# Two state-space layers: decay clamp moved from VectorE to ScalarE, the masked product of C and B in one pass, half of the products one weight piece later

## The chip, the cores and the metric

The kernel runs on one core of a Trainium2 chip. The metric is the device time of one execution in microseconds (us). The kernel before takes 2148.89 us, the median of three runs (2148.83 to 2150.71).

Engines are named as the profile names them: PE is TensorE's matmul, PEld its weight load, DVE is VectorE, ACT is ScalarE, POOL is GpSimd, SP is SyncE.

## The reference

A network of four layers on 256 tokens of width 1024, in 32-bit floats. Each layer is a gated feed-forward block, a mixer, and a second feed-forward block, with a layer norm behind each. The mixers of layers 0 to 3 are: state space, attention with a forget gate, block attention, state space. Only the state-space mixer (`mamba2_mixer`) is touched here:

```python
zxbcdt = x @ w_in
z, xbc, dt = split(zxbcdt)                     # 2048, 2048 + 2*4*128, 32 columns
xbc = silu(causal_conv4(xbc) + conv_b)         # then xs, b, c
dt = softplus(dt + dt_bias);  a = -exp(a_log)
# per group g of 4, with 8 heads of 64 columns, state size 128
a_cs = cumsum(dt * a)
decay_in[l, s] = exp(a_cs[l] - a_cs[s])  for s <= l, else 0
cb = c[l] . b[s]
y = (cb * decay_in) @ (x * dt)                 # the diagonal terms
y = y + x * d_skip
y = y * silu(z)
y = y * rsqrt(mean(y^2 over the group) + eps) * norm_w
out = y @ w_out
```

The 256 tokens are one chunk for the reference. The kernel computes them as two halves of 128: the second half gets its own triangle (the diagonal terms) and the contribution of the first half through the state of the first half (the off-diagonal term).

## The kernel before, in words

**Tiles and streams.** Every weight matrix is cut into pieces of 128x2048 floats. SP loads a piece into a raw tile, ACT copies it to a rounded tile `wh` and DVE subtracts that from the raw tile to give the rest `wl` (`split`, L122 to L124, four passes of 128x512 on each engine for each piece). Each product is three matmuls, `wh` by `xh`, `wl` by `xh` and `wh` by `xl` (L148 to L150). The 256 tokens are two streams of 128, t=0 (the first tokens) and t=1 (the second tokens). Both use the same piece, t=1 two pieces after t=0 (`LAG` is 2).

**The state-space mixer.** `ssm` is a generator for one stream. Its pieces come in the order X0 Z0 X1 Z1 O0 X2 Z2 X3 O1 Z3 O2 O3: X is three pieces of the group (two for x, one for B and C), Z and O are two. Stage functions are attached to pieces by `at(i, f, ...)` and run in the code behind the matmuls of piece i:

- `stage_x`, `stage_bc`: the projection is copied out of PSUM (L445 on ACT, L453 on DVE), transposed (L158), put behind the three older tokens (L447, L455 on DVE), and, in the second stream, convolved (L427 on ACT, L431 on DVE) and put through Silu (L434 on ACT).
- `stage_back`: transposes back (L464), the products with dt, the skip and the decay to the end (L469 on DVE), the product of B and C on PE (L478), masked by the triangle on DVE (L481). In the second stream the tile holds two products side by side, of which the second is not masked and is copied by ACT (L483).
- `stage_off`: the off-diagonal matmul (L489), from the first half's state, and its decay (L491, L494 on DVE).
- `stage_m`, twice for each group and stream: a row of cumulated decays is spread over 128 partitions by a DMA, four DVE passes add the partition's own negative value and cut at zero (L502), ACT takes the exponential (L503), DVE multiplies by the masked product (L504). The tiles are named `mt`, five of them.
- `stage_y`: eight matmuls of 64 columns (L512, sixteen records in the profile), added to the skip term on DVE (L514).
- `stage_z`, `stage_n`, `stage_a`: Silu of z on ACT (L519), product (L524), square with a sum on ACT (L526), the scale on DVE and POOL (L527, L528), the scaled result on DVE (L529), transposes (L158) and the split into `ah` and `al` (L123, L124) for the O pieces.

**What sets the order.** The two streams are interleaved piece by piece, and a scheduler orders the instructions of each engine when the program is built; `tc.keep_in_program_order` holds an instruction in the place of the code. Each engine then runs its list in order and waits on semaphores. PSUM has two tiles each of three kinds. Those named `tp` hold transposes and the product of B and C, those named `gu` and `ga` projections and diagonal terms, and those named `acc0` and `acc1` the output sums. ACT loads a table of functions (ACT_TABLE_LOAD) where the next function is not in the one that it has.

Of the kernel before, what the change touches and what calls it, by code (L numbers as in the profile page):

```python
# [7 lines left out]
F32 = mybir.dt.float32  # L8
FR = mybir.dt.float32r
BF = mybir.dt.bfloat16  # L10
AF = mybir.ActivationFunctionType
ALU = mybir.AluOpType
# [37 lines left out]
def build(tc, x, wst, ln_g, ln_b, sm_dt, sm_rows, sm_conv, sm_nw, fx_f, fx_b, out, plan=None):  # L50
    nc = tc.nc
    ctx = ExitStack()
    cpool = ctx.enter_context(tc.tile_pool(name="const", bufs=1))
# [13 lines left out]
    def T():  # L67
        return ps_t.tile([128, 512], F32, name="tp")
# [7 lines left out]
    def tmp(cols, tag, bufs, dt=F32):  # L76
        return spool.tile([128, cols], dt, name=tag, tag=tag, bufs=bufs)
# [6 lines left out]
    K = {}  # L84

    def consts():
        if K:
            return
        up = tmp(128, "t1", 5)
        make_upper_triangular(nc, up, val=1.0, diag=True)  # L90
        lo = tmp(128, "t1", 5)
        make_lower_triangular(nc, lo, val=1.0, diag=False)
        K["tri"] = cpool.tile([128, 128], FR, name="tri")
        nc.vector.tensor_copy(K["tri"], up)
        K["ntri"] = cpool.tile([128, 128], FR, name="ntri")
        nc.vector.tensor_scalar_mul(K["ntri"], up, -1.0)
        K["sel"] = cpool.tile([128, 32], FR, name="sel")
        nc.vector.tensor_add(K["sel"], ident[:, 0:32], ident[:, 32:64])
        K["strict"] = cpool.tile([128, 128], FR, name="strict")
        nc.vector.tensor_copy(K["strict"], lo)  # L100
        K["idb"] = cpool.tile([128, 128], BF, name="idb")
        nc.vector.tensor_copy(K["idb"], ident)
        K["mlo"] = cpool.tile([128, 128], BF, name="mlo")
        nc.vector.tensor_scalar_mul(K["mlo"], lo, NEG)
        K["mup"] = cpool.tile([128, 128], BF, name="mup")
        nc.vector.tensor_sub(up, up, ident)
        nc.vector.tensor_scalar_mul(K["mup"], up, NEG)
# [251 lines left out]
    def ssm_small(j):  # L359
        if j in ssms:  # L360
            return ssms[j]
        consts()
        s = St()
        s.dt = small_w(sm_dt[j], 32)
        s.rows = tmp(96, "rows", 1)
        nc.sync.dma_start(s.rows, bc(sm_rows[j:j + 1, :], 96))
        s.conv = spool.tile([128, 24, 5], F32, name="conv", bufs=1)
        nc.sync.dma_start(s.conv, sm_conv[j])
        s.na = tmp(32, "na", 1)
        nc.scalar.activation(s.na, s.rows[:, 32:64], AF.Exp)  # L370
        nc.vector.tensor_scalar_mul(s.na, s.na, -1.0)
        s.nw = {}
        s.xb, s.cv, s.B, s.xe = {}, {}, {}, {}
        ssms[j] = s
        return s
# [7 lines left out]
    def ssm(st, j):  # L383
        t = st.t
        s = ssm_small(j)
        d = St()
# [12 lines left out]
        def stage_cum():  # L399
            ps = T()  # L400
            nc.tensor.matmul(ps[:, :128], d.h, K["tri"], start=True, stop=False)
            nc.tensor.matmul(ps[:, :128], d.l, K["tri"], start=False, stop=True)
            cr = tmp(128, "cumr", 2)
            nc.scalar.activation(cr[:32], ps[:32, :128], AF.Copy)
            d.cum = dpool.tile([32, 128], F32, name="cums")
            nc.sync.dma_start(d.cum, cr[:32])
            ps = T()
            for n, mat in enumerate(("tri", "strict")[:2 - t]):
                nc.tensor.matmul(ps[:, n * 32:n * 32 + 32], K[mat], d.h[:, :32], start=True, stop=False)
                nc.tensor.matmul(ps[:, n * 32:n * 32 + 32], K[mat], d.l[:, :32], start=False, stop=True)  # L410
            d.ncum = tmp(32, "ncum", 2)
            nc.vector.tensor_scalar_mul(d.ncum, ps[:, :32], -1.0)
            if t == 0:
                d.de = tmp(32, "de", 1)
                nc.scalar.activation(d.de, ps[:, 32:64], AF.Exp)
                nc.vector.tensor_mul(d.de, d.de, d.dt)
            else:
                d.ec = tmp(32, "ec", 1)
                nc.scalar.activation(d.ec, ps[:, :32], AF.Exp)
# [16 lines left out]
        bank, cbs, zss, y1s = {}, {}, {}, {}  # L436
# [13 lines left out]

        def stage_bc(g):
            bcs = tmp(256, "t1", 5)
            nc.vector.tensor_copy(bcs, bank.pop(g)[:, :256])  # L453
            tp = transposes(bcs, 2)
            nc.vector.tensor_copy(s.xb[g][:, 4:6, 3 + t * 128:131 + t * 128], tp[:, :256].rearrange("p (a b) -> p a b", a=2))  # L455
            if t == 1:
                conv(g, 4, 6)

        def stage_back(g):
            cv = s.cv[g]  # L460
            h8 = slice(g * 8, g * 8 + 8)
            tp = T()
            for k in range(4):
                nc.tensor.transpose(tp[:, k * 128:(k + 1) * 128], cv[:, k, mine], ident)  # L464
            tp8 = tp.rearrange("p (a b) -> p a b", a=8)

            def times(tag, rows, bufs):
                o = tmp(512, tag, bufs)
                nc.vector.tensor_mul(o.rearrange("p (a b) -> p a b", a=8), tp8,  # L469
                                     rows[:, h8].unsqueeze(2).to_broadcast([128, 8, 64]))  # L470
                return o
            xds[g] = (times(f"xdt{t}", d.dt, 1 + t), times("xD", s.rows[:, 64:96], 2))
            if t == 0:
                s.xe[g] = times("xe", d.de, 1)
            tp = T()
            for n in range(1 + t):
                B = cv[:, 4, mine if n == 0 else slice(0, 128)]
                nc.tensor.matmul(tp[:, n * 128:(n + 1) * 128], B, cv[:, 5, mine], start=True, stop=True)  # L478
            cb = tmp(256, "t1", 5)
            nn = (1 + t) * 128  # L480
            nc.vector.tensor_mul(cb[:, :128], tp[:, :128], K["tri"].bitcast(F32))  # L481
            if t:
                nc.scalar.activation(cb[:, 128:], tp[:, 128:256], AF.Copy)  # L483
            cbs[g] = cb
            mts[g] = []

        def stage_off(g):
            yo = G()
            nc.tensor.matmul(yo, cbs[g][:, 128:256], s.xe[g], start=True, stop=True)  # L489
            w = tmp(512, "t2", 4)  # L490
            nc.vector.tensor_mul(w.rearrange("p (a b) -> p a b", a=8), yo.rearrange("p (a b) -> p a b", a=8),  # L491
                                 d.ec[:, g * 8:g * 8 + 8].unsqueeze(2).to_broadcast([128, 8, 64]))
            xD = xds[g][1]
            nc.vector.tensor_add(xD, xD, w)  # L494

        def stage_m(g, qd):
            e = spool.tile([128, 4, 128], F32, name="mt", bufs=5)
            h0 = g * 8 + qd * 4
            row = d.cum[h0:h0 + 4, :].rearrange("h l -> (h l)").unsqueeze(0)
            nc.sync.dma_start(e.rearrange("p a b -> p (a b)"), row.to_broadcast([128, 512]))  # L500
            for h in range(4):
                nc.vector.tensor_scalar(e[:, h], e[:, h], d.ncum[:, h0 + h:h0 + h + 1], 0.0, op0=ALU.add, op1=ALU.min)  # L502
            nc.scalar.activation(e, e, AF.Exp)  # L503
            nc.vector.tensor_mul(e, e, cbs[g][:, 0:128].unsqueeze(1).to_broadcast([128, 4, 128]))  # L504
            mts[g].append(e)

        def stage_y(g):
            mt, (xd, xD) = mts.pop(g), xds.pop(g)
            y = G()
            for h in range(8):  # L510
                c64 = slice(h * 64, h * 64 + 64)
                nc.tensor.matmul(y[:, c64], mt[h // 4][:, h % 4], xd[:, c64], start=True, stop=True)  # L512
            y1s[g] = tmp(512, "t2", 4)
            nc.vector.tensor_add(y1s[g], y, xD)  # L514

# [20 lines left out]
        def at(i, f, *a):  # L536
            post.setdefault(i, []).append((f, a))
# [6 lines left out]
        for g in range(N_GRP):  # L544
            b = where["X", g, 2]
            at(b - 1, stage_x, g)
            at(b, stage_bc, g)
            c = b + (LAG if t == 0 else 0)
            at(c + 1, stage_back, g)
            at(c + 2, stage_m, g, 0)  # L550
            at(c + 2, stage_m, g, 1)
            if t == 1:
                at(c + 2, stage_off, g)
            z = where["Z", g, 1]
            at(z, stage_z, g)
            iy = c + 3
            at(iy, stage_y, g)
            n = max(iy, z)
            at(n, stage_n, g)
            at(min(n + 1, where["O", g, 0] - 1), stage_a, g)  # L560
        first_o = where["O", 0, 0]
        for i, (kind, g, n) in enumerate(pieces):
            if (kind == "X" and n != 1) or (kind == "Z" and n == 0):
                ps = bank[g] = GA(int(kind == "Z" or n == 2)) if i < first_o else G()
# [358 lines left out]
```

## Time and profile before

| | before |
|---|---|
| median of three runs | 2148.89 us |
| the profiled execution | 2147.68 us |
| its span in the profile | 2145.9 us |
| PE busy | 2111.0 us (98 %) |
| DVE busy | 1493.1 us (70 %) |
| ACT busy | 1121.4 us (52 %) |
| TensorE clock granted | 0.999 of full speed |

The profiled execution took 2147.68 us, 1.8 us more than the span that its trace covers, and lies 1.2 us below the median. Matmul busy time overlaps from one to the next, so PE's idle time is read better from the table of what PE waited for than from the busy share. In rows of a timeline the first number is the start, the second the duration; `x4` joins four instructions; what stands in brackets is the idle time of the engine before the row and what ended it.

### The profile page before, as it was taken

What the parts mean: (1) busy time and instruction counts of PE and PEld (TensorE: products, weight loads), DVE (VectorE), ACT (ScalarE), POOL (GpSimd) and SP (SyncE); (2) the same over time, 40 slices, a digit from 0 to 9 for tenths busy, and PEclk for the clock granted to TensorE, in tenths of its full rate; (3) what the DMA queues carried; (4) which work ended last, traced back from release to release, by engine and by line L of the source; (5) the groups of instructions that cost most, each with busy time, mean ns of one, the idle gap of its engine ahead of it and who ended that gap; (6) DMA issues with size and microseconds to landing.
All of it is one profiled execution on the core that took longest, in us unless ns stands there. A gap on an engine that the chain in (4) does not pass through costs nothing.

```text
span 2145.9 us, 29868 instructions
## 1 busy us (share of the span) xinstructions
PE 2111.0 (98%) x10346; PEld 1745.7 (81%) x10346; DVE 1493.1 (70%) x2975; ACT 1121.4 (52%) x2298; POOL 476.0 (22%) x858
## 2 busy tenths in 40 slices
PE   8999999999999999999999999999999999999998
PEld 7888878788888888788888887788888888787886
DVE  6657999855765575765675575765576679998655
ACT  6444776544544455544544455544445447665442
POOL 2331000233143200043233300034223310001331
PEclk9999999999999999999999999999999999999999
DMA  9665544666576643466666653376666655446662
GB/s 322 228 228 189 192 167 154 229 234 223 188 261 230 216 167 118 148 233 224 219 229 229 225 200 138 118 248 235 223 216 236 230 203 175 165 173 208 236 228 94
DMA packets 225927, 438.81 MB, mean 204 GB/s; under 512 B 20464, under 2 KB 20976, under 8 KB 225776
## 3 DMA queue, kind: packets, MB, share of 16 engines
q1 hardware_dynamic: 197616, 394.92, 51.3%
q0 software_dynamic: 28160, 41.99, 6.6%
q8 instruction: 81, 1.33, 0.3%
q14 instruction: 70, 0.57, 0.1%
HBM read 414.74 MB, written 22.09 MB: 204 GB/s over the span
## 4 chain that ended last, share of the span: by engine, by line
PE 91%; DVE 4%; ACT 2%; DMA 1%; issue 1%; POOL 0%; DVEq 0%; SPq 0%; ACTq 0%
PE gu L150 16%; PE gu L148 16%; PE gu L149 15%; PE acc L150 9%; PE acc L148 9%; PE acc L149 9%; PE ga L148 4%; PE ga L149 3%; PE ga L150 3%; PE tp L158 3%; DVE wl L124 1%; PE gu L512 1%; DMA raw<-in_w_dram 1%; PE gu L694 1%; DVE mt L502 1%
## 5 line engine op out<-in xcount | busy, mean ns | idle before, releaser
L124 DVE TENSOR_TENSOR wl<-raw,wh 128x512 fp32r<-128x512 f32 x1408 | 887.8, 683 | 361.4 <-ACT wh L123 360.1
L123 ACT ACTIVATE wh<-raw 128x512 fp32r<-128x512 f32 x1408 | 775.2, 621 | 522.2 <-PE gu L150 216.0
L148 PE MATMUL gu<-wh,xh 128*128 128x512 f32 (+1 forms) x1600 | 619.3, 387 | 5.7 <-ACT t L519 2.7
L150 PE MATMUL gu<-wh,xl 128*128 128x512 f32 (+1 forms) x1600 | 617.0, 386 | 0.9 <-DVE xl L124 0.9
L149 PE MATMUL gu<-wl,xh 128*128 128x512 f32 (+1 forms) x1600 | 616.9, 386 | 0.0
L246 POOL DMA_DIRECT2D aT<-turn x640 | 348.3, 551 | 500.0 <-issue 286.4
L148 PEld LDWEIGHTS gu<-wh,xh 128*128 128x128 f32 x1600 | 300.9, 188 | 68.1 <-DVE t L272 3.7
L150 PE MATMUL acc<-wh,al 128*128 128x512 f32 x896 | 352.5, 394 | 0.0
L149 PE MATMUL acc<-wl,ah 128*128 128x512 f32 x896 | 352.4, 393 | 0.0
L148 PE MATMUL acc<-wh,ah 128*128 128x512 f32 x896 | 351.3, 393 | 0.0
L150 PEld LDWEIGHTS gu<-wh,xl 128*128 128x128 f32 x1600 | 300.7, 188 | 61.8 <-DVE xl L124 2.1
L149 PEld LDWEIGHTS gu<-wl,xh 128*128 128x128 f32 x1600 | 300.8, 188 | 59.5 <-issue 0.5
L272 DVE TENSOR_TENSOR t<-t,gu 128x256 f32<-128x256 f32 x176 | 73.6, 418 | 191.3 <-ACT t L270 191.3
L270 ACT ACTIVATE t<-gu 128x256 f32<-128x256 f32 x176 | 67.7, 384 | 258.9 <-PE gu L150 241.1
L150 PEld LDWEIGHTS acc<-wh,al 128*128 128x128 f32 x896 | 168.3, 188 | 37.5 <-DVE al L124 2.3
L148 PEld LDWEIGHTS acc<-wh,ah 128*128 128x128 f32 x896 | 168.3, 188 | 34.9 <-issue 0.5
L149 PEld LDWEIGHTS acc<-wl,ah 128*128 128x128 f32 x896 | 168.3, 188 | 34.6 <-issue 1.3
L242 POOL DMA_DIRECT2D turn<-tb x160 | 90.3, 565 | 321.5 <-DVE tb L240 302.3
L148 PE MATMUL ga<-wh,xh 128*128 128x512 f32 (+1 forms) x448 | 159.6, 358 | 1.4 <-ACT xh L123 1.4
L150 PE MATMUL ga<-wh,xl 128*128 128x512 f32 (+1 forms) x448 | 156.4, 350 | 0.0
L149 PE MATMUL ga<-wl,xh 128*128 128x512 f32 (+1 forms) x448 | 156.1, 349 | 0.0
L190 POOL TENSOR_TENSOR rstd<-ve,mhalf 128x1 f32<-128x1 f32 x24 | 22.6, 942 | 481.5 <-DVE ve L188 481.5
(171 smaller groups left out, 1641.0 us busy)
## 6 DMA issues: line engine op xcount, KB each, us to landing
raw<-in_w_dram SPq DMA_DIRECT2D x351, 1024.0 KB, 5.3
turn<-tb POOLq DMA_DIRECT2D x160, 128.0 KB, 3.3
aT<-turn POOLq DMA_DIRECT2D x640, 32.0 KB, 4.0
mt<-cums SPq DMA_DIRECT2D x32, 256.0 KB, 4.7
gb<-in_ln_g_dram SPq DMA_DIRECT2D x12, 512.0 KB, 4.5
gb<-in_ln_b_dram SPq DMA_DIRECT2D x12, 512.0 KB, 6.0
nw<-in_sm_nw_dram SPq DMA_DIRECT2D x8, 256.0 KB, 5.3
h<-in_x_dram SPq DMA_DIRECT2D x4, 256.0 KB, 4.5
```

The source lines that it names most:

```text
L123: a = nc.scalar.activation(wh, raw, AF.Copy)
L124: return a, nc.vector.tensor_sub(wl, raw, wh.bitcast(F32))
L148: nc.tensor.matmul(o, xh, wh, start=start, stop=False)
L149: nc.tensor.matmul(o, xh, wl, start=False, stop=False)
L150: nc.tensor.matmul(o, xl, wh, start=False, stop=stop)
L158: nc.tensor.transpose(tp[:, j * 128:(j + 1) * 128], src[:, j * 128:(j + 1) * 128], ident)
L190: nc.gpsimd.tensor_tensor(rstd, ve, mhalf, op=ALU.pow)
L242: nc.gpsimd.dma_start(dr, b.rearrange("p q k t -> p (q k t)"))
L246: nc.gpsimd.dma_start(aT[32 * q:32 * q + 32].rearrange("p i k t -> p i (k t)"), dv[q])
L270: nc.scalar.activation(sg, gu[:, :256], AF.Silu)
L272: nc.vector.tensor_mul(a, sg, gu[:, 256:])
L502: nc.vector.tensor_scalar(e[:, h], e[:, h], d.ncum[:, h0 + h:h0 + h + 1], 0.0, op0=ALU.add, op1=ALU.min)
```

## The change

It edits `consts` and five of `ssm`'s stage functions. A constant `cut` of 128x256 (triangle, then ones) lets one DVE pass mask and copy the product of B and C for both streams, and ACT's copy goes. `cums` holds the positive cumulated decays. The clamp of DVE, `min(row - cum, 0)`, becomes ACT's `relu(cum - row)`, and the exponential gets a scale of -1. `stage_bc`'s copy out of PSUM goes from DVE to ACT. The off-diagonal matmul and the first diagonal matmul are held in the order of the code. For the second stream and groups 0 to 2, `stage_m` and `stage_y` are attached one piece later.

```diff
+        K["cut"] = cpool.tile([128, 256], F32, name="cut")
+        nc.vector.tensor_copy(K["cut"][:, 0:128], up)
+        nc.vector.memset(K["cut"][:, 128:256], 1.0)
...
-            d.ncum = tmp(32, "ncum", 2)
-            nc.vector.tensor_scalar_mul(d.ncum, ps[:, :32], -1.0)
+            d.cums = tmp(32, "ncum", 2)
+            nc.vector.tensor_copy(d.cums, ps[:, :32])
...
-            nc.vector.tensor_copy(bcs, bank.pop(g)[:, :256])
+            nc.scalar.activation(bcs, bank.pop(g)[:, :256], AF.Copy)
...
-            nc.vector.tensor_mul(cb[:, :128], tp[:, :128], K["tri"].bitcast(F32))
-            if t:
-                nc.scalar.activation(cb[:, 128:], tp[:, 128:256], AF.Copy)
+            nc.vector.tensor_mul(cb[:, :nn], tp[:, :nn], K["cut"][:, :nn])
...
-            nc.tensor.matmul(yo, cbs[g][:, 128:256], s.xe[g], start=True, stop=True)
+            tc.keep_in_program_order(nc.tensor.matmul(yo, cbs[g][:, 128:256], s.xe[g], start=True, stop=True))
...
-                nc.vector.tensor_scalar(e[:, h], e[:, h], d.ncum[:, h0 + h:h0 + h + 1], 0.0, op0=ALU.add, op1=ALU.min)
-            nc.scalar.activation(e, e, AF.Exp)
+                nc.scalar.activation(e[:, h], e[:, h], AF.Relu, scale=-1.0, bias=d.cums[:, h0 + h:h0 + h + 1])
+            nc.scalar.activation(e, e, AF.Exp, scale=-1.0)
...
-                nc.tensor.matmul(y[:, c64], mt[h // 4][:, h % 4], xd[:, c64], start=True, stop=True)
+                ins = nc.tensor.matmul(y[:, c64], mt[h // 4][:, h % 4], xd[:, c64], start=True, stop=True)
+                if h == 0:
+                    tc.keep_in_program_order(ins)
...
-            at(c + 2, stage_m, g, 0)
-            at(c + 2, stage_m, g, 1)
+            late = int(t == 1 and g < 3)
+            at(c + 2 + late, stage_m, g, 0)
+            at(c + 2 + late, stage_m, g, 1)
...
-            iy = c + 3
+            iy = c + 3 + late
```

Lines of the changed kernel from L98 on carry a number higher by three at first (L148 is L151, L158 is L161, L478 is L481, L489 is L490, L512 is L513), since `cut` takes three lines and the mask's copy gives two back.

In ACT's order the table loads number 40 before and 52 after, six more in each of the two state-space layers.

What the change moves on the engines is seen in the order of their instructions. A row is line, operation, out<-in and shape; numbers behind a name tell tiles of one name apart, and they differ between the two programs.

The first place is PE in layer 0, group 0. The rows named `ga` with 256 columns are the B and C projection of the next group; `tp<-cv` is the product of B and C, whose input `cv` comes from the convolution's Silu. Before:

```order
L149 MATMUL ga_2334<-wl_2220,xh0_1813 128x256
L150 MATMUL ga_2334<-wh_2219,xl0_1814 128x256
L148 MATMUL ga_2334<-wh_2219,xh0_1813 128x256
L149 MATMUL ga_2334<-wl_2220,xh0_1813 128x256
L150 MATMUL ga_2334<-wh_2219,xl0_1814 128x256
L148 MATMUL ga_2334<-wh_2219,xh0_1813 128x256
L149 MATMUL ga_2334<-wl_2220,xh0_1813 128x256
L478 MATMUL tp_2252<-cv_1920 128x128
L464 MATMUL tp_2268<-ident_78,cv_1920 128x128 x4
L478 MATMUL tp_2277<-cv_1920 128x128 x2
L150 MATMUL ga_2334<-wh_2219,xl0_1814 128x256
```

After:

```order
L153 MATMUL ga_2219<-wh_1936,xl1_1978 128x512
L151 MATMUL ga_2336<-wh_2222,xh0_1816 128x256
L152 MATMUL ga_2336<-wl_2223,xh0_1816 128x256
L153 MATMUL ga_2336<-wh_2222,xl0_1817 128x256
L481 MATMUL tp_2255<-cv_1923 128x128
L467 MATMUL tp_2271<-ident_78,cv_1923 128x128 x4
L151 MATMUL ga_2336<-wh_2222,xh0_1816 128x256
L152 MATMUL ga_2336<-wl_2223,xh0_1816 128x256
L153 MATMUL ga_2336<-wh_2222,xl0_1817 128x256
L151 MATMUL ga_2336<-wh_2222,xh0_1816 128x256
L152 MATMUL ga_2336<-wl_2223,xh0_1816 128x256
```

Eleven matmuls of the 256-column projection stood ahead of the first product (the fence shows the last seven), and three do now.

The second place is PE in layer 0, group 1. `tp<-cv ... x2` is the second stream's product of B and C, `gu<-xe,t1` the off-diagonal matmul, for which `t1` is the masked product; `acc0` are output sums. Before:

```order
L150 MATMUL ga_2616<-wh_2373,xl1_1975 128x512
L149 MATMUL acc0_2804<-wl_2554,ah_2520 128x512
L150 MATMUL acc0_2804<-wh_2553,al_2521 128x512
L464 MATMUL tp_2670<-ident_78,cv_2324 128x128 x4
L478 MATMUL tp_2679<-cv_2324 128x128 x2
L489 MATMUL gu_2754<-xe_2652,t1_2682 128x512
L148 MATMUL gu_2725<-wh_2619,xh0_1813 128x512
```

After:

```order
L152 MATMUL acc0_2789<-wl_2450,ah_2595 128x512
L481 MATMUL tp_2681<-cv_2326 128x128 x2
L153 MATMUL acc0_2789<-wh_2449,al_2596 128x512
L151 MATMUL acc0_2789<-wh_2449,ah_2595 128x512
L152 MATMUL acc0_2789<-wl_2450,ah_2595 128x512
L153 MATMUL acc0_2789<-wh_2449,al_2596 128x512
L151 MATMUL acc0_2789<-wh_2542,ah_2599 128x512
L152 MATMUL acc0_2789<-wl_2543,ah_2599 128x512
L490 MATMUL gu_2739<-xe_2654,t1_2684 128x512
L151 MATMUL gu_2726<-wh_2621,xh0_1816 128x512
L152 MATMUL gu_2726<-wl_2622,xh0_1816 128x512
```

The off-diagonal matmul stood directly behind the product, and now six matmuls of the output sums stand between.

The same group on DVE, from the masked product of the second stream to the decay of the off-diagonal term (`t<-gu,ec`) and the row behind it. Before:

```order
L481 TENSOR_TENSOR t_2682<-tp,tri 128x128
L124 TENSOR_TENSOR wl<-raw,wh 128x512 x3
L502 TENSOR_SCALAR mt<-mt,ncum 128x128 x16
L504 TENSOR_TENSOR mt<-mt,t_2656 128x512 x2
L504 TENSOR_TENSOR mt<-mt,t_2682 128x512 x2
L491 TENSOR_TENSOR t_2756<-gu,ec 128x512
L124 TENSOR_TENSOR wl<-raw,wh 128x512
```

After:

```order
L484 TENSOR_TENSOR t_2684<-tp,cut 128x256
L127 TENSOR_TENSOR wl<-raw,wh 128x512 x3
L505 TENSOR_TENSOR mt<-mt,t_2658 128x512 x2
L492 TENSOR_TENSOR t_2741<-gu,ec 128x512
L127 TENSOR_TENSOR wl<-raw,wh 128x512
L495 TENSOR_TENSOR xD<-xD,t_2741 128x512
L127 TENSOR_TENSOR wl<-raw,wh 128x512 x3
L517 TENSOR_TENSOR t_2779<-gu,xD 128x512
L527 TENSOR_TENSOR t_2779<-t_2779,t_2564 128x512
L505 TENSOR_TENSOR mt<-mt,t_2684 128x512
```

Sixteen clamps and two of the four products stood ahead of the decay of the off-diagonal term and now do not: the clamps are ACT's, and the second stream's two products come after it.

The third place is PE in layer 0, group 2. `gu<-xdt1` is the second stream's diagonal product, and `tp<-ident,t2` the transposes of the first stream's normalised result. Before:

```order
L149 MATMUL gu_3248<-wl_2968,xh1_1974 128x512
L150 MATMUL gu_3248<-wh_2967,xl1_1975 128x512
L148 MATMUL gu_3248<-wh_2967,xh1_1974 128x512
L149 MATMUL gu_3248<-wl_2968,xh1_1974 128x512
L150 MATMUL gu_3248<-wh_2967,xl1_1975 128x512
L512 MATMUL gu_3322<-xdt1_3151,mt_3225 128x64 x4
L512 MATMUL gu_3322<-xdt1_3151,mt_3233 128x64 x4
L158 MATMUL tp_3363<-ident_78,t2_3294 128x128 x4
L148 MATMUL gu_3248<-wh_3030,xh1_1974 128x512
```

After:

```order
L153 MATMUL gu_3232<-wh_2968,xl1_1978 128x512
L151 MATMUL gu_3232<-wh_2968,xh1_1977 128x512
L152 MATMUL gu_3232<-wl_2969,xh1_1977 128x512
L153 MATMUL gu_3232<-wh_2968,xl1_1978 128x512
L153 MATMUL acc1_2632<-wh_3163,al_2849 128x512
L151 MATMUL gu_3232<-wh_3031,xh1_1977 128x512
L152 MATMUL gu_3232<-wl_3032,xh1_1977 128x512
L161 MATMUL tp_3346<-ident_78,t2_3278 128x128 x4
L153 MATMUL gu_3232<-wh_3031,xl1_1978 128x512
L151 MATMUL gu_3232<-wh_3031,xh1_1977 128x512
```

The second stream's eight diagonal matmuls stood ahead of those transposes and now come behind them; two more projection matmuls and one of the output sum stand there instead, fifteen large matmuls where there were twelve, counted from the first stream's own diagonal product.

## Rows read from the trace of the kernel before

**Rows 1.** Page, busy time, share of the span and instructions of each engine.

```profile
PE 2111.0 (98%) x10346; PEld 1745.7 (81%) x10346; DVE 1493.1 (70%) x2975; ACT 1121.4 (52%) x2298; POOL 476.0 (22%) x858
```

**Rows 2.** What PE waited for, whole run: total us, times, longest.

```profile
PE gu L489 <- ACT t L483: 2.9, 2, 1.4
PE gu L148 <- ACT t L519: 2.7, 2, 1.4
PE gu L512 <- DVE t L491: 2.1, 2, 1.1
...
PE tp L158 <- DVE t L529: 1.7, 6, 0.5
...
PE gu L148 <- DVE sm L527: 1.0, 2, 0.5
...
PE tp L158 <- DVE al L124: 0.5, 2, 0.2
```

**Rows 3.** Layer 0's mixer by stretch: busy of five engines, clock, DMA, GB/s.

```profile
300.00:320.00 20.00, 18.63 (x99) 15.71 (x99) 19.69 (x54) 17.69 (x30) 0.00 (x0) 1.00 0.44 164
...
sum 151.00, PE 145.59 PEld 124.05 DVE 139.42 ACT 100.63 POOL 5.76; mean PE 24.27 PEld 20.67 DVE 23.24 ACT 16.77 POOL 0.96
```

**Rows 4.** Timeline of DVE in group 1 of layer 0.

```profile
276.30 0.28 DVE L481 TENSOR_TENSOR t<-tp,tri 128x128 f32<-128x128 f32 x1
...
278.30 3.23 DVE L502 TENSOR_SCALAR mt<-mt,ncum 128x128 f32<-128x128 f32 x16
281.44 2.49 DVE L504 TENSOR_TENSOR mt<-mt,t 128x512 f32<-128x512 f32 x4
283.85 0.68 DVE L491 TENSOR_TENSOR t<-gu,ec 128x512 f32<-128x512 f32 x1
```

**Rows 5.** Timeline of PE in the same group.

```profile
276.94 1.12 PE L489 MATMUL gu<-xe,t 128*128 128x512 f32 x2 [1.44 <-ACT t L483]
...
284.59 2.00 PE L512 MATMUL gu<-xdt,mt 128*128 128x64 f32 x16 [1.06 <-DVE t L491]
```

**Rows 6.** Timeline of ACT in group 2 of layer 0.

```profile
308.83 2.08 ACT L427 ACTIVATE cv<-xb,conv 128x256 f32<-128x256 f32 x4 [0.66 <-DVE xb L447]
...
312.22 0.60 ACT L519 ACTIVATE t<-gu 128x512 f32<-128x512 f32 x1
...
329.92 0.60 ACT L519 ACTIVATE t<-gu 128x512 f32<-128x512 f32 x1
```

**Rows 7.** Timeline of PE at the first of these.

```profile
312.87 0.50 PE L148 MATMUL gu<-wh,xh 128*128 128x512 f32 x1 [1.37 <-ACT t L519]
```

**Rows 8.** Timeline of ACT in group 0 of layer 0.

```profile
233.64 1.28 ACT L434 ACT_TABLE_LOAD   x1
234.94 0.63 ACT L434 ACTIVATE cv<-cv 128x512 f32<-128x512 f32 x1
```

**Rows 9.** Timeline of PE in group 0 of layer 0.

```profile
234.42 0.28 PE L148 MATMUL ga<-wh,xh 128*128 128x256 f32 x1
...
235.74 0.38 PE L478 MATMUL tp<-cv 128*128 128x128 f32 x2
```

**Rows 10.** Groups of ACT by line and shape: busy us, mean ns, idle before.

```profile
L427 ACT ACTIVATE cv<-xb,conv 128x256 f32<-128x256 f32 x48 | 25.3, 591 | 5.5 <-DVE xb L447 4.1 <-DVE xb L455 1.3
...
L659 ACT ACTIVATE mt<-tp,rs 128x128 f32<-128x128 f32 x32 | 11.3, 366 | 14.1 <-DVE rs L655 14.1
...
L483 ACT ACTIVATE t<-tp 128x128 f32<-128x128 f32 x8 | 2.2, 272 | 3.9 <-DVE t L481 3.9
```

**Rows 11.** Timeline of DVE at group 2's first normalisation, layer 0.

```profile
335.73 0.69 DVE L514 TENSOR_TENSOR t<-gu,xD 128x512 f32<-128x512 f32 x1 [1.31 <-PE gu L512]
...
339.02 0.75 DVE L529 SCALAR_TENSOR_TENSOR t<-t,sm,nw 128x512 f32<-128x512 f32 x1 [0.67 <-POOL sm L528]
```

**Rows 12.** Timeline of PE beside it.

```profile
333.80 1.89 PE L512 MATMUL gu<-xdt,mt 128*128 128x64 f32 x16
335.53 0.39 PE L158 MATMUL tp<-ident,t 128*128 128x128 f32 x2
...
340.25 0.61 PE L158 MATMUL tp<-ident,t 128*128 128x128 f32 x4
```

## The prediction

> **What bounds the kernel now.** I read the page's busy times first. PE is busy for 98 % of the span, DVE for 70 %, ACT for 52 % [rows 1]. The number of PE's matmuls does not change, so the change can only win or lose in PE's idle time, and the second view is the list of what PE waited for. Six of its rows belong to the two state-space layers: 2.9 us for ACT's copy L483, 2.7 us for the Silu of z (L519), 2.1 us for L491, 1.7 us for the normalised result (L529), 1.0 us for L527 and 0.5 us for a split [rows 2]. Most come twice, once in each layer. They sum to 10.9 us, which is all that the change can give back: 0.5 % of the time.
>
> The third view, by stretch, says why these waits are there. In the 151 us of layer 0's mixer from 197 to 348 us DVE is busy for 139.4 us (92 %) and ACT for 100.6 us (67 %) [rows 3]. The fourth view, DVE's timeline in group 1, shows the queue: 16 clamps, then four products, then L491, each starting before the end of the one ahead [rows 4].
>
> **The load that moves, per layer.** DVE gives 64 clamps at 3.23/16 = 0.20 us, 12.9 us, and 8 copies of 256 columns at about 0.4 (between 0.28 us for 128 columns and 0.69 us for 512 [rows 4, 11]), 3.2 us. It gets 4 masks of double width at +0.14, 0.6 us. So 139.4 - 15.5 = 124 us, 82 %. No row shows a Relu with scale and bias on 128x128. The nearest are a plain copy of that size at 272 ns, an activation with a pointer operand on that size at 366 ns, and one with two pointers on twice the width at 591 ns [rows 10]. Consecutive ones overlap: four L427 take 2.08 us, 0.50 apart, 0.1 less than their mean [rows 6, 10]. So a Relu costs between 0.17 (the copy less 0.1) and 0.49; I take 0.27, the 366 less 0.1. ACT gets 64 x 0.27 = 17.3 us, 8 copies at about 0.3 = 2.4 us and six more table loads at 1.28 [rows 8] = 7.7 us, and loses 4 copies (0.7 us): 100.6 + 26.7 = 127 us, 84 %. With the ends of the Relu it is 121 or 141 us. Both engines would then be fuller than ACT is now and emptier than DVE is now, so I expect no new bound over the whole stretch; the single places decide.
>
> For that one activation the Trainium skill, "ScalarE: Activation LUTs", section "What ACT_TABLE_LOAD costs", gives about 280 ns plus 0.833 ns a column with a bias pointer, and 93 ns of overlap: 387 - 93 = 294 ns as an estimate, 1.5 us more per layer than my sum. Its 1283 ns for a table load is what the trace shows.
>
> **Wait for L483, 2.9 us.** PE waits 1.44 us ahead of L489 [rows 5], until DVE's mask at 276.30 [rows 4] and ACT's copy behind it are done. After the change ACT is out of this chain, and PE has six large matmuls at 0.24 us there, 1.4 us. (0.24 from twelve of them between the transposes at 335.53 and 340.25, less 1.73 us for the eight small ones [rows 12].) PE is free at 276.94 - 1.44 = 275.50, and would arrive at 276.9; the wider mask ends at about 276.3 + 0.42 = 276.7. The wait goes: -2.9 us.
>
> **Wait for L491, 2.1 us.** PE's diagonal product waits 1.06 us [rows 5], because its PSUM tile is the one that L491 reads, and L491 stands at the end of DVE's queue. 16 clamps (3.2 us) and two products (1.2 us) leave that queue. The first stream's products then wait for eight Relus and two exponentials on ACT, 8 x 0.27 + 1.2 = 3.4 us, no later than the 16 clamps let them be. PE comes to the tile about twelve large matmuls earlier by the new order, 2.9 us. The relief of 4.4 us against 2.9 + 1.06 leaves 0.4 us of slack: -2.1 us.
>
> **Wait for L527, 1.0 us.** It is a buffer's release behind the second stream's L514, and that moves by a piece: -1.0 us.
>
> **Waits for L529 and the split, 2.2 us.** Two of the six L529 waits, 0.5 us each, are in group 0, where DVE's relief comes in time. The others belong to the chain through ACT's square and POOL's power, which no edit shortens. I leave 1.2 us of the 2.2: -1.0 us.
>
> **Wait for the Silu of z, 2.7 us.** PE stands 1.37 us at 312.87 [rows 7]. ACT's Silu begins at 312.22; ahead of it L427 waited 0.66 us for DVE's copy L447 [rows 6], which stood behind clamps. That 0.66 goes, the rest stays: 2.7 becomes 1.4 us, -1.3 us.
>
> **New: group 0's first product of B and C.** Eight of the eleven 256-column matmuls ahead of it go behind it. Eleven lie between 234.42 and 235.74 [rows 9], 0.12 us each, so PE comes 0.96 us earlier, at 234.8. The Silu that it needs ends at 234.94 + 0.63 = 235.57, behind a table load [rows 8], and no edit brings it forward. PE waits 0.8 us in each layer, with the projection queued behind it, +1.6 us. The cover that goes is those eight matmuls.
>
> **New: group 2's first normalisation.** Between the end of the diagonal product at 335.53 and the transposes at 340.25 [rows 12] DVE and ACT need until 339.02 + 0.75 = 339.77 [rows 11], 4.24 us, and PE waits for nothing. Afterwards fifteen matmuls and two transposes stand there, 15 x 0.24 + 0.1 = 3.7 us. PE waits about 0.6 us in each layer, with the projection of the z columns and the second diagonal product behind it: +1.2 us.
>
> The DMAs that spread the decays are issued in another order among the weight loads on SP, where a wait for a free `mt` tile holds the loads behind it. DVE's clamps began without idle time [rows 4], so the rows came early; I cost this at nothing, with the loaded-ahead weights as cover. If that cover goes, a late weight costs ACT, DVE and PE alike what the tile was late.
>
> **The sum.** Of 10.9 us stay 1.2 + 1.4 = 2.6; 1.6 + 1.2 are new: 5.4 us. The gain is 5.5 us. The profiled execution took 2147.68 us, 1.2 us below the median, so it would take 2142.2, and the median 2148.89 - 5.5 = 2143.4 us.
>
> **Rivals.**
> 1. All of the idle time goes, since DVE is relieved by more than each place shows and the two new waits don't come: 2148.9 - 10.9 = 2138 us. For it speaks that the list of DVE's relief (15.5 us per layer) is larger than every wait. Against it, two of the waits are for ACT. Chance 0.15.
> 2. Waits for ACT take the place of those for DVE. From 308.83 to 329.92 ACT has no idle time in the trace [rows 6], 17.69 of 20 us with its overlaps [rows 3]; Relus and Copies put in there push the Silu of z and the weight casts by about what DVE gave. The Silu's wait then stays at 2.7 instead of 1.4, and 1 us comes at two more places of each layer: 5.4 + 1.3 + 4 = 10.7 us of idle time where there were 10.9, or 2148.7 us. Chance 0.22.
> 3. Slower: ACT's table loads become the bound. Relu has no load of its own, but between Silu and Exp pieces each is now in another order, six more loads a layer. In that gapless stretch two loads, 2.6 us, fall on a chain which PE waits for, in each group where the held diagonal product cannot be passed by the projection behind it. At four such places 4 x 2.6 = 10.4, less 5.5: +4.9, 2153.8 us; all twelve loads on the path would give 2148.9 - 5.5 + 15.4 = 2158.8. It decides from a second place on: two places cancel the gain. Against it, ACT still has 16 % free. Chance 0.13. The Trainium skill, same page, section "Rules for kernel authors", speaks for this rival: relu, like add and max, belongs on VectorE. No run here has yet weighed the two engines.
>
> **How the numbers follow.** The forecast has 0.50, with 2141 to 2146 us as its own range, from half a microsecond either way on four of the terms. What a measurement of this kernel can tell from no change is about 0.2 %, 4.3 us: faster is below 2144.6, slower above 2153.2. Of the forecast 0.40 lies below, 0.10 within; rival 1 is faster, rival 2 within, rival 3 slower: faster 0.55, same 0.32, slower 0.13. The range runs from 2138 to 2152, which leaves out rival 3 and the far end of rival 1.
>
> **What would show it.** In the profile after: no row of PE's waits for the mask at L490, none for L492 at the diagonal product; about 1.4 us for the Silu of z; new rows of 1.6 us at L481 for ACT's Silu L437 and of about 1.2 us more at the transposes for L532; DVE at 124 and ACT at 127 us in the same stretch; a Relu at 0.27 us. The prediction is wrong if PE waits for ACT's `mt` or `wh` in the state-space layers, or if the waits there sum to more than 8 or less than 3 us.

## The result: 14.7 us faster, where 5.5 were forecast

The changed kernel takes 2135.38 us, the median of six runs (2134.62 to 2137.98); the kernel before took 2150.07 in six runs beside them (2148.83 to 2150.75). The ratio is 0.9935, 95 % interval 0.9923 to 0.9948. The sign was right, the size was not, and the time lies below the stated range (2138 to 2152). Two executions far off all others (10118.03 us of one variant, 2633.28 us of the kernel before) are left out of the medians below.

The profiled execution took 2134.62 us, 13.1 less than the one of before. Its busy times answer to [rows 1]:

```profile
PE 2108.4 (99%) x10346; PEld 1745.6 (82%) x10346; DVE 1464.4 (69%) x2833; ACT 1172.6 (55%) x2446; POOL 474.0 (22%) x858
```

DVE has 28.7 us less over the two layers, 14.4 each (15.5 forecast), and ACT 51.2 us more, 25.6 each (26.7 forecast). The loads were sized well. One Relu takes 391 ns, and they follow each other 0.29 us apart, four in 1.27 us (0.27 forecast). By line and shape, and in ACT's timeline:

```profile
L503 ACT ACTIVATE mt<-mt,ncum 128x128 f32<-128x128 f32 x128 | 42.7, 391 | 0.0
```
```profile
226.49 1.27 ACT L503 ACTIVATE mt<-mt,ncum 128x128 f32<-128x128 f32 x4
```

The waits were not sized well. Of the six rows of [rows 2], only these two have a successor in what PE waits for after the change, whole run:

```profile
PE gu L151 <- ACT t L522: 1.2, 2, 0.6
PE tp L161 <- DVE t L532: 0.8, 2, 0.4
```

The Silu of z stays with 1.2 us (1.4 forecast). The second row is the new wait for group 2's normalised result, 0.42 us in each layer (0.6 forecast). That makes 2.0 us where there were 10.9. PE's idle time in the 151 us of layer 0 answers to [rows 3]:

```profile
260.00:280.00 20.00, 19.98 (x101) 15.95 (x100) 19.70 (x40) 19.74 (x37) 0.12 (x1) 1.00 0.46 171
280.00:300.00 20.00, 20.00 (x116) 17.33 (x115) 15.72 (x29) 19.04 (x48) 1.48 (x2) 1.00 0.66 212
300.00:320.00 20.00, 19.42 (x107) 16.45 (x106) 17.98 (x38) 19.63 (x35) 0.12 (x1) 1.00 0.45 171
...
sum 151.00, PE 149.88 PEld 128.28 DVE 132.80 ACT 129.13 POOL 5.78; mean PE 24.98 PEld 21.38 DVE 22.13 ACT 21.52 POOL 0.96
```

PE is idle for 1.1 us there, for 5.4 before. (DVE shows 133 us and not 124 in this stretch. PE runs ahead there, with 870 matmuls where there were 840, and work of later pieces has moved into it.)

All of the gain lies in the two layers: PE's 1000th matmul starts at 223.0 us before and 223.6 after, the 2200th at 460.8 and 454.3, the 8600th at 1779.3 and 1772.8, the 9800th at 2014.6 and 2001.3. That is 7.1 us in layer 0 and 6.8 in layer 3, 13.9 in all, more than all of the 10.9 us that I had called the most that could come. A second profiled execution of the changed kernel gives 13.9 by the same starts.

### The profile page after: what moved, and what is told of

The parts are those of the page before. It is cut to its first block, busy times and chain, and to the rows that moved or that the text cites. A ratio compares the mean times of both kernels' runs of the same rounds, so it can differ in the third digit from the quotient of the medians.

```text
span 2132.7 us, 29860 instructions
## 1 busy us (share of the span) xinstructions
PE 2108.4 (99%) x10346; PEld 1745.6 (82%) x10346; DVE 1464.4 (69%) x2833; ACT 1172.6 (55%) x2446; POOL 474.0 (22%) x858
## 4 chain that ended last, share of the span: by engine, by line
PE 94%; DVE 2%; ACT 2%; DMA 1%; issue 1%; SPq 0%; POOL 0%; DVEq 0%; ACTq 0%
PE gu L151 16%; PE gu L153 16%; PE gu L152 16%; PE acc L153 9%; PE acc L151 9%; PE acc L152 9%; PE ga L151 4%; PE ga L152 4%; PE ga L153 4%; PE tp L161 3%; PE gu L513 1%; DVE wl L127 1%; PE gu L698 1%; ACT wh L126 1%; DMA raw<-in_w_dram 0%
## 5 line engine op out<-in xcount | busy, mean ns | idle before, releaser
L151 PE MATMUL gu<-wh,xh 128*128 128x512 f32 (+1 forms) x1600 | 618.9, 387 | 1.3 <-ACT t L522 1.2
L151 PE MATMUL acc<-wh,ah 128*128 128x512 f32 x896 | 352.8, 394 | 0.0
L151 PEld LDWEIGHTS gu<-wh,xh 128*128 128x128 f32 x1600 | 301.1, 188 | 62.3 <-ACT t L522 1.6
L151 PEld LDWEIGHTS acc<-wh,ah 128*128 128x128 f32 x896 | 168.3, 188 | 35.9 <-issue 1.5
L151 PE MATMUL ga<-wh,xh 128*128 128x512 f32 (+1 forms) x448 | 159.8, 357 | 1.4 <-ACT xh L126 1.4
```

What stands on the lines that cost most here:

```text
L151: nc.tensor.matmul(o, xh, wh, start=start, stop=False)
```

## The experiments

Theory 1, formed on that trace: VectorE's queue was late all through the two layers, and the gain is its relief. Theory 2: the order (later products, held matmuls) made it. Theory 3: it takes both.

**The clamp alone on ScalarE**

```diff
 (before)
...
-                nc.vector.tensor_scalar(e[:, h], e[:, h], d.ncum[...], 0.0, op0=ALU.add, op1=ALU.min)
-            nc.scalar.activation(e, e, AF.Exp)
+                nc.scalar.activation(e[:, h], e[:, h], AF.Relu, scale=-1.0, bias=d.cums[...])
+            nc.scalar.activation(e, e, AF.Exp, scale=-1.0)
```

> The kernel before with the clamp moved to ScalarE and nothing else (four more table loads in ScalarE's order). Theory 1, the gain is VectorE's relief, since every wait that went away in the change, those at the handover to the feed-forward block included, ends in a VectorE queue that was late: this edit alone takes 12.9 of the 15.5 us of relief per layer, so it gives about 8 to 11 of the 14.7 us: 2139 to 2142. Theory 2, the gain is the later place of the second tokens' products and the held matmuls: 0 to 3 us, 2147 to 2150. Theory 3, it takes both, since ScalarE alone in the old order delays the copy L483 and the Silu of z: within 2 us of before, or slower.

Measured: 2135.48 us (five runs), ratio 0.9938 (0.9926 to 0.9951) against 2149.42 for the kernel before. This one edit gives the whole gain within the noise, 13.9 us, more than theory 1 had for it.

**The later place alone**

```diff
 (before)
+            late = int(t == 1 and g < 3)
-            at(c + 2, stage_m, g, 0)
-            at(c + 2, stage_m, g, 1)
+            at(c + 2 + late, stage_m, g, 0)
+            at(c + 2 + late, stage_m, g, 1)
...
-            iy = c + 3
+            iy = c + 3 + late
```

> The kernel before with the second tokens' products and diagonal matmuls one piece later and nothing else (four more table loads). Theory 1 (VectorE's relief): the order takes the diagonal matmuls' wait for L491 (2.1 us) and that for L527 (1.0 us), 2 to 4 us: 2146 to 2148. Theory 2 (the order): 9 us or more, under 2141. Theory 3 (both are needed): within 2 us of before.

Measured: 2153.73 us (eleven runs), ratio 1.0021 (1.0012 to 1.0030): slower. Theory 2 had 9 us or more of gain, and falls. The first stream's normalised result is what comes late (in layer 0 at 291 us, in group 1), as in my step on group 2, but by much more while DVE is full. What PE waited for:

```profile
PE tp L158 <- DVE t L529: 5.4, 4, 2.6
```

Behind the longest of these waits, one in each layer, the granted clock fell, which lost about 3.4 us each time by the sum of the last section. That is 6.8 us, more than the 4.3 us by which this variant is slower: with the clock at 1.00 the later place alone would be about neutral or slightly faster, an estimate.

**The change without the clamp's move, and without the later place**

```diff
 (after, first kernel)
...
-                nc.scalar.activation(e[:, h], e[:, h], AF.Relu, scale=-1.0, bias=d.cums[...])
-            nc.scalar.activation(e, e, AF.Exp, scale=-1.0)
+                nc.vector.tensor_scalar(e[:, h], e[:, h], d.ncum[...], 0.0, op0=ALU.add, op1=ALU.min)
+            nc.scalar.activation(e, e, AF.Exp)
 (after, second kernel)
-            late = int(t == 1 and g < 3)
-            at(c + 2 + late, stage_m, g, 0)
-            at(c + 2 + late, stage_m, g, 1)
+            at(c + 2, stage_m, g, 0)
+            at(c + 2, stage_m, g, 1)
...
-            iy = c + 3 + late
+            iy = c + 3
```

> The changed kernel with the clamp back on VectorE, all else as changed (44 table loads instead of 52). Theory 1: most of the gain is lost, 2143 to 2147. Theory 2: most of it stays, 2135 to 2139. Theory 3: all is lost, 2147 or more.

Measured: 2150.34 us (eleven runs), ratio 1.0003 (0.9994 to 1.0013). All is lost, which was theory 3's number; but the clamp alone keeps the whole gain, so that theory falls too. Of the 15 us between this variant and the change about 8.5 are the clock's, which fell in both layers (5.1 and 3.4 us, last section); what is left by this sum, 6.5 us, goes to DVE's load and its waits.

> The changed kernel with the second tokens' products and diagonal matmuls at their old place, all else as changed (40 table loads instead of 52). Theory 1: most of the gain stays, 2136 to 2140, and the twelve table loads that are saved cost nothing as ScalarE is not the bound. Theory 2: most is lost, 2144 or more. Theory 3: all is lost, 2147 or more.

Measured: 2134.82 us (five runs), ratio 0.9933 (0.9920 to 0.9945). The later place is worth nothing once DVE is relieved.

**VectorE's time put back, without the chain**

```diff
 (the clamp alone)
...
                 nc.scalar.activation(e[:, h], e[:, h], AF.Relu, scale=-1.0, bias=d.cums[...])
+                nc.vector.tensor_scalar(K["scr"], K["tri"].bitcast(F32), d.cums[...], 0.0, op0=ALU.add, op1=ALU.min)
```

> The clamp on ScalarE alone (2135.5 us), and beside each Relu one VectorE pass of the old clamp's form into a scratch tile that nothing reads, so that VectorE is as loaded as before and the new chain through ScalarE stays. Theory 1a, it is VectorE's time that counts: the gain goes, 2147 to 2151. Theory 1b, it is the chain (the clamp waited in VectorE's queue behind weight splits, and ScalarE takes it at once): most of it stays, 2136 to 2141.

Measured: 2150.33 us (eleven runs), ratio 1.0006 (0.9997 to 1.0015). Passes that nobody reads take the whole gain back, about 1.7 us of it by one fall of the clock: it is VectorE's time that counts (1a), not the clamp's place in a chain (1b). In the 151 us DVE (the third busy time, columns as in [rows 3]) is at 140.64 us, where it had been at 139.4, and PE at 146.81, where the change has 149.88:

```profile
197.00:348.00 151.00, 146.81 (x841) 124.63 (x840) 140.64 (x338) 116.23 (x238) 5.82 (x10) 1.00 0.53 180
```

The waits that come back are for ACT's copy and, behind the mixer, for the layer norm on DVE, which the clamp alone has not in its list:

```profile
PE tp L159 <- DVE h L199: 4.1, 2, 2.0
PE gu L490 <- ACT t L484: 2.9, 2, 1.4
```

One rival stays open beside VectorE's time: the scheduler orders every variant anew. In group 1 of layer 0 no matmul stands between the second stream's product of B and C and the off-diagonal matmul in the kernel before, seven do with the clamp alone, and none with the filler. PE's rows at that matmul, with the clamp alone and with the filler:

```profile
275.96 1.12 PE L489 MATMUL gu<-xe,t 128*128 128x512 f32 x2 [0.46 <-ACT t L483]
```
```profile
278.45 1.12 PE L490 MATMUL gu<-xe,t 128*128 128x512 f32 x2 [1.43 <-ACT t L484]
```

At this place the order goes with the load and is worth about 2 us over both layers (waits of 0.9 and 2.9 us). No run holds the order fixed while VectorE's load changes.

**Half of the relief, and a sixth of it**

```diff
 (before, first kernel)
...
+                if qd:
                     nc.vector.tensor_scalar(e[:, h], e[:, h], d.ncum[...], 0.0, op0=ALU.add, op1=ALU.min)
+                else:
+                    nc.scalar.activation(e[:, h], e[:, h], AF.Relu, scale=-1.0, bias=d.cums[...])
-            nc.scalar.activation(e, e, AF.Exp)
+            nc.scalar.activation(e, e, AF.Exp, scale=1.0 if qd else -1.0)
 (before, second kernel)
...
-            nc.vector.tensor_copy(bcs, bank.pop(g)[:, :256])
+            nc.scalar.activation(bcs, bank.pop(g)[:, :256], AF.Copy)
...
-            nc.vector.tensor_mul(cb[:, :128], tp[:, :128], K["tri"].bitcast(F32))
-            if t:
-                nc.scalar.activation(cb[:, 128:], tp[:, 128:256], AF.Copy)
+            nc.vector.tensor_mul(cb[:, :nn], tp[:, :nn], K["cut"][:, :nn])
```

> The kernel before with the clamp of every first quad of heads on ScalarE and that of every second one on VectorE: half of the relief, 6.5 us per layer (and one more VectorE pass of 32 columns for each half of the tokens). Theory 1a with a proportional gain: about 7 us, 2142. If VectorE only has to fall under what the single places stand: more than half, 2135 to 2139. Theory 1b (the chain): the second quad still waits in VectorE's queue, 2145 or more.

Measured: 2142.68 us (seven runs), ratio 0.9971 (0.9960 to 0.9981): 6.3 us.

> The kernel before with the one-pass mask and stage_bc's copy on ScalarE, and nothing else: 2.6 us of relief per layer, and ScalarE's copy is out of the chain to the off-diagonal matmul. Theory 1a proportional: 2 to 3 us, 2146 to 2147. If the wait for that copy (2.9 us) goes on top: 2143 to 2145. Theory 1b: only that wait goes, 2146.

Measured: 2144.98 us (eleven runs), ratio 0.9980 (0.9971 to 0.9988): 4.0 us. PE's wait for L483 (2.9 us) is gone there and the others in the two mixers are nearly as they were (the one for L491 is 2.7 us, the one for the Silu of z 1.9), so this fits the second of its expectations. With 2.6, 6.5, 12.9 and 15.5 us of relief per layer the gains are 4.0, 6.3, 13.9 and 14.7 us (13.3 when the change was measured again).

This looks like a gain in proportion, but the two small ones hold losses by the clock. In the profiled executions it fell in both layers with half of the clamps, and in layer 3 with the mask and the copy, 1.7 us each time. By PE's own starts the four gain 4.4, 5.0, 13.0 and 13.9 us there; with the clock's loss put back that is 6.1, 8.4, 13.0 and 13.9, an estimate. The first microseconds of relief then bring more than the last, and the gain is at an end with the clamp, when PE has little left to wait for.

**More work for ScalarE**

```diff
 (the clamp alone, first kernel; the second has the added line under "if h == 0:")
...
                 nc.scalar.activation(e[:, h], e[:, h], AF.Relu, scale=-1.0, bias=d.cums[...])
+                nc.scalar.activation(K["scr"], K["tri"].bitcast(F32), AF.Relu, scale=-1.0, bias=d.cums[...])
```

> The clamp on ScalarE alone, and beside each Relu a second one into a scratch tile that nothing reads: 64 x 0.295 = 19 us more of ScalarE in each of the two layers, which then has more to do there than VectorE had before. If ScalarE is far from being the bound (theory 1a and 1b): 2136 to 2139. If ScalarE is close to it, as my third rival had it: 2146 or more.

Measured: 2151.60 us (eleven runs), ratio 1.0009 (1.0000 to 1.0018). More work on ScalarE can take the whole gain, as my third rival had it by another way. About 5.1 us of the 16 are the clock's, which fell in both layers, and the off-diagonal matmul of group 1 stands directly behind the product again, as in the kernel before. Waits of that kernel:

```profile
PE gu L490 <- ACT t L484: 3.3, 2, 1.7
PE tp L159 <- DVE t L531: 3.2, 10, 0.6
...
PE gu L151 <- DVE xl L125: 1.4, 2, 0.7
```

> The clamp on ScalarE alone, and beside the first Relu of each quad a second one into a scratch tile that nothing reads: 16 x 0.295 = 4.7 us more of ScalarE per layer, a quarter of the earlier filler. If ScalarE has a margin and the whole filler ran past it: 2135 to 2138. If ScalarE is a bound already, with a loss in proportion (16 us for 19 us per layer): 2139 to 2140 or more.

Measured: 2136.50 us (six runs), ratio 0.9936 (0.9916 to 0.9956). Against the kernel before, ACT's busy time per layer grew by 18.9 us with the clamp alone, 25.6 in the change, 31.9 here and 42.8 with the whole filler (halves of the differences of the page's busy times):

```profile
PE 2110.3 (99%) x10346; PEld 1746.7 (82%) x10346; DVE 1470.4 (69%) x2847; ACT 1185.1 (56%) x2474; POOL 477.9 (22%) x858
```
```profile
PE 2116.2 (98%) x10346; PEld 1748.6 (81%) x10346; DVE 1469.3 (68%) x2847; ACT 1206.9 (56%) x2566; POOL 479.3 (22%) x858
```

The first is the quarter, the second the whole filler. The quarter grew by 13.0 us per layer over the clamp alone, and not by the 4.7 of its expectation, since its order of ACT also has twelve table loads more (56, where the clamp alone has 44), 7.7 us per layer. So 31.9 us more for ScalarE cost about 1 us (the change, measured beside it, took 2135.33), and 42.8 cost the whole gain. ACT's share of the 151 us does not show where the limit lies. It is 129.13 us in the change, and with the quarter and the whole filler

```profile
sum 151.00, PE 150.04 PEld 127.78 DVE 133.88 ACT 130.93 POOL 5.78; mean PE 25.01 PEld 21.30 DVE 22.31 ACT 21.82 POOL 0.96
```
```profile
sum 151.00, PE 146.20 PEld 122.99 DVE 126.77 ACT 130.00 POOL 6.90; mean PE 24.37 PEld 20.50 DVE 21.13 ACT 21.67 POOL 1.15
```

With the whole filler PE is behind and later work has left the stretch. In the change ACT is busy for 58.4 of the 60 us from 260 to 320 (rows of the first section), and PE is idle there for 0.6 us: an engine can be nearly full where its results are not late.

**Is there a better version?**

```diff
 (after, the version without the later place, and without the copy on ScalarE)
-            late = int(t == 1 and g < 3)
-            at(c + 2 + late, stage_m, g, 0)
-            at(c + 2 + late, stage_m, g, 1)
+            at(c + 2, stage_m, g, 0)
+            at(c + 2, stage_m, g, 1)
...
-            iy = c + 3 + late
+            iy = c + 3
 (the second of them, besides)
-            nc.scalar.activation(bcs, bank.pop(g)[:, :256], AF.Copy)
+            nc.vector.tensor_copy(bcs, bank.pop(g)[:, :256])
```

> The changed kernel once more, beside the next one on one chip: 2135 to 2136 by either theory, as a yardstick.

> The changed kernel without the later place, 12 table loads fewer. If the 12 loads (15.4 us of ScalarE over both layers) are hidden, as the first pair says: within 1 us of the changed kernel. If they stand on the path in part: 2 us or more below it, 2133 or less.

> Clamp on ScalarE, one-pass mask, both matmuls held; stage_bc's copy stays on VectorE and the later place is left out. It is the version to which the experiments point: the copy L483 that the clamp alone leaves PE waiting for (0.9 us) goes, and ScalarE is spared 16 copies and the later place's table loads. If only idle time that is left can be won: 2133.5 to 2135.5.

Measured on one chip, medians: 2135.33, 2134.82 and 2135.50 us, with ratios 0.9931 (0.9914 to 0.9949), 0.9929 (0.9911 to 0.9947) and 0.9932 (0.9912 to 0.9951). They can't be told apart. The version without the later place has twelve table loads fewer, 15.4 us of ACT, and is 0.6 and 0.5 us lower in the two comparisons: the loads are hidden, as in my sum, and not on a chain as rival 3 had it.

## Why the prediction was wrong, step by step

The step that failed is the one that I called "all that the change can give back": the 10.9 us of six rows. It was too small in two ways: it left out waits behind the mixer, and it counted a wait at its row alone. On top of that I gave too much of it back in new and remaining waits. The waits that remain sum to 2.0 us, under the 3 us that the prediction named as a sign of being wrong. Of the rivals the first comes closest (all idle time goes, since DVE is relieved by more than each place shows), but its 2138 us rested on the same 10.9. Over both layers, against 13.9 us by PE's own starts:

| term | forecast | measured |
|---|---|---|
| waits for L483, L491, L527 | -6.0 | -6.0 |
| L529 and the split (2.2) | -1.0 | -2.2 |
| Silu of z (2.7) | -1.3 | -1.5 |
| new, group 0's product of B and C | +1.6 | 0 |
| new, group 2's normalisation | +1.2 | +0.8 |
| waits behind the mixer | 0 | -2.3 |
| cost of a wait beyond its row | 0 | -2.7 (the rest) |

**Remaining waits that did not remain.** Of L529 and the split I left 1.2 us, for the chain through ACT's square and POOL's power. None of it is in the list after the change; what stands there is group 2's new wait. Which part of that chain came earlier I have not followed.

**Waits that I had put outside.** Two rows of the list of before, over the whole run, belong in part to the handover from the mixer to the feed-forward block; I had left them out. In layer 0, from 348 to 430 us, PE waited in the kernel before:

```profile
PE gu L148 <- DVE t L272: 0.8, 1, 0.8
PE gu L150 <- DVE xl L124: 0.5, 1, 0.5
```

In layer 3 it is 0.5 and 0.5. After the change there is none, and with the clamp alone there is none either. The second is a split among the layer norm's passes in DVE's list. The first comes by the SP queue. I had cost that queue at nothing, but only for the DMAs that spread the decays; this is another DMA. The layer norm's two weight rows go to a tile that is free only when the layer norm before has ended (L198 on DVE), and their DMA, held in the order of the code, stood in SP's queue ahead of the weight loads. Before, in SP's waits and ACT's timeline:

```profile
SPq L118 <- DVE h L198: 10.0, 1, 10.0
```
```profile
411.49 2.19 ACT L123 ACTIVATE wh<-raw 128x512 fp32r<-128x512 f32 x4 [7.22 <-DMA raw<-in_w_dram]
```

DVE's split waits for that copy, and the product L272, for which PE waits until 415.04, stands behind it:

```profile
412.15 2.50 DVE L124 TENSOR_TENSOR wl<-raw,wh 128x512 fp32r<-128x512 f32 x4 [2.13 <-ACT wh L123]
414.57 0.41 DVE L272 TENSOR_TENSOR t<-t,gu 128x256 f32<-128x256 f32 x1
```

After, in SP's waits and ACT's timeline:

```profile
SPq L121 <- DVE h L201: 3.0, 1, 3.0
```
```profile
404.93 2.19 ACT L126 ACTIVATE wh<-raw 128x512 fp32r<-128x512 f32 x4 [5.31 <-PE gu L153]
```

A DVE that is late at the mixer's end is late at the layer norm, holds SP for 10.0 us, and ACT waits 7.22 us for a weight. Afterwards SP is held for 3.0 us, the weight rows are issued at 398.10 instead of 402.18, and ACT waits for PE and no longer for a load. The chain is read from one trace of each kernel; that waits of this place hang on DVE's load is shown by the filler, which brings 4.1 us of them back.

**A wait costs more than its row.** Around the 1.37 us of [rows 7], PE's timeline of before has:

```profile
311.22 0.28 PE L150 MATMUL gu<-wh,xl 128*128 128x256 f32 x1
...
313.20 0.39 PE L149 MATMUL gu<-wl,xh 128*128 128x512 f32 x1
```

From 311.22 to the start at 312.87 are 1.65 us, where 0.12 is usual; and the next one starts 0.33 us later, where 0.23 is usual. Together 1.63 us for a row of 1.37. The idle time counts from the modelled end of the last matmul, and the first ones behind a gap come slowly. The 2.7 us of the table are a remainder; that they are all of this kind is argued from such pairs, not shown one by one.

**New wait at the product of B and C: absent.** I had argued from one row that no edit brings the Silu forward. After the change, in the timelines of ACT and PE:

```profile
234.61 0.63 ACT L437 ACTIVATE cv<-cv 128x512 f32<-128x512 f32 x1
```
```profile
235.23 0.28 PE L153 MATMUL ga<-wh,xl 128*128 128x256 f32 x1
235.35 0.44 PE L481 MATMUL tp<-cv 128*128 128x128 f32 x2
```

The Silu ends at 235.24 and PE comes at 235.35, without waiting. PE is 0.6 us later here than before by its start, and the Silu 0.3 us earlier than the 235.57 of [rows 8], since the copy L445 that stood ahead of its table load (0.58 us) stands behind it now. (PE's start is later by the same 0.6 us at its 1000th matmul, ahead of this place.) The order of ACT shows this; my step took only PE's order into account.

**What was right.** The masked product is in time: DVE's pass ends at 273.48 + 0.41 = 273.89, and the off-diagonal matmul starts at 274.37 after six others, without a wait. The diagonal product does not wait either:

```profile
273.48 0.41 DVE L484 TENSOR_TENSOR t<-tp,cut 128x256 f32<-128x256 f32 x1
```
```profile
274.37 1.02 PE L490 MATMUL gu<-xe,t 128*128 128x512 f32 x2
...
278.00 1.89 PE L513 MATMUL gu<-xdt,mt 128*128 128x64 f32 x16
```

Both answer to [rows 5]. These two terms, the one for L527, the Silu of z and group 2's wait came out within 0.4 us. For group 2 the rows of [rows 12] give 2.99/12 = 0.249 us a matmul, and not 0.24; with it fifteen take 3.74 us and the wait is 0.40 in each layer, near the measured 0.42. The waits for L483 and L491 are gone or smaller with the clamp alone too (0.9 us and none), so the held matmuls and the later place were not needed for most of it.

**The price of a Relu, and the engine for it.** The Trainium skill, "ScalarE: Activation LUTs", section "What ACT_TABLE_LOAD costs", gave 294 ns for a Relu in a row as an estimate from its figures, and the trace has 0.29 us. The section "Rules for kernel authors" would leave a relu to VectorE; here the move is worth the whole gain, since VectorE was at 92 % and ScalarE at 67 % of the stretch. The measurement decides, for this balance.

## What to carry to other kernels

Here the relief of an engine that was 92 % busy in a stretch was worth more than the waits that named it there. In such a case add the waits behind the stretch, and what the queues that its end releases (here SP's, behind the layer norm's weights) hold back. But a busy share alone does not say that an engine is late: ScalarE was busy for 58.4 of 60 us in the change, where PE had 0.6 us of idle time. Test the load by itself, with passes that nobody reads, and look at the clock and at the new order before the times are compared. And look where the receiving engine's margin ends: here 32 us more per layer cost about 1 us, and 43 the whole gain.

## Not expected of the hardware

In some of the variants a longer idle time of PE was followed by a lower clock. In the change without the clamp's move, PE waits once for 2.77 us in layer 0, and the granted clock then falls. The columns are those of [rows 3]:

```profile
289.39 1.12 PE L161 MATMUL tp<-ident,t 128*128 128x128 f32 x4 [2.77 <-DVE t L532]
```
```profile
284.00:288.00 4.00, 2.62 (x12) 1.81 (x10) 3.10 (x12) 2.93 (x6) 0.39 (x1) 1.00 0.61 158
288.00:292.00 4.00, 2.48 (x11) 2.11 (x11) 3.56 (x7) 3.77 (x8) 0.55 (x1) 0.57 0.57 213
292.00:296.00 4.00, 4.00 (x20) 4.00 (x20) 1.50 (x4) 1.76 (x4) 0.00 (x0) 0.50 0.29 100
296.00:300.00 4.00, 4.00 (x23) 3.91 (x23) 3.56 (x8) 1.01 (x3) 0.93 (x1) 0.65 0.85 292
```

0.50 is the lower of the two levels, 1.2 GHz. Taken as time less the granted share, the three stretches from 288 lose 4 x (0.43 + 0.50 + 0.35) = 5.1 us, more than the wait itself; in layer 3 it is 3.4 us, behind a wait of 2.79. So the 15 us between the change and this variant are not all DVE's load. The clock also fell in the variants with the later place alone, with either filler in full and with half of the clamps, behind waits of 1.7 to 2.6 us, and in the one with the one-pass mask and the copy behind one of 1.34 us. In the kernel before it stayed at 1.00 behind a wait of 1.44 us [rows 5], so the length of one wait does not tell it alone. Two executions of one kernel, the change without the later place, say so most plainly. Outside the two layers PE waits in both for 0.69 and then for 1.02 us, the latter until 768.8 us, and the clock stays in the first execution and falls in the second:

```profile
768.00:772.00 4.00, 3.23 (x26) 3.16 (x27) 3.48 (x15) 1.57 (x4) 0.00 (x0) 1.00 1.02 385
```
```profile
768.00:772.00 4.00, 3.17 (x16) 3.17 (x17) 3.12 (x12) 1.64 (x5) 0.00 (x0) 0.66 1.02 388
```

In the changed kernel it stayed at 1.00, as in the kernel before, so the comparison of these two does not rest on it.
